# Second norm's sum of squares: the seventh tile's squares join the running sum

## The chip, the cores and the metric

The kernel runs on one core of one Trainium2 chip. The core has five engines that run side by side and meet through semaphores: TensorE (PE; its weight loads are shown apart, as PEld), VectorE (DVE), ScalarE (ACT), GpSimd (POOL) and SyncE (SP), which issues the DMAs here. The metric is the device time of one execution in microseconds; the time of a kernel is the median of its runs.

## The reference: what is computed

One decoder layer of depth 1 on 1024 tokens with 1024 features: an RMS norm, sliding-window attention with sinks, a residual add, a second RMS norm, a squared-ReLU MLP (hidden width 4096), another residual add and a final norm. What the change touches is the second norm, the one ahead of the MLP:

```python
def rms_norm(x, g):
    xf = x.astype(jnp.float32)
    y = xf * lax.rsqrt(jnp.mean(xf * xf, axis=-1, keepdims=True) + RMS_EPS)
    return (y * g.astype(jnp.float32)).astype(x.dtype)
...
        h = h + mix
        h = h + squared_relu_mlp(rms_norm(h, mlp_norm[i]), mlp_w_up[i], mlp_w_down[i])
```

For each token the mean of its 1024 squared features is wanted.

## The kernel before, in words

Features lie on the 128 partitions, tokens along the free axis. The residual `h` is eight tiles of 128 features by 1024 tokens, `h[0]` to `h[7]`, and is worked on in two halves of 512 tokens: half 0 and half 1. Big matrix products are made with operands split into a high and a low part, so one 128x512 block of a product is a run of matmuls in groups of three.

Around the change the program goes like this. The second part of the attention's output projection is made block by block (`oblock(m, hf)`, 12 matmuls each): first m = 0 to 7 for half 0, then m = 0 to 7 for half 1. After each block `oadd` (VectorE) adds it to `h[m]`, and `square` (ScalarE) writes the squares of that 128x512 piece into a tile `sq2_m_hf` (`sq` in the profile). The squares have to be summed over 1024 features, that is over the eight tiles and over the 128 partitions of each. Over tiles they are partly summed by adds into the first tile's squares: on VectorE for half 0, on GpSimd for half 1. Before the change the tiles 1 to 5 are added in this way, and the tiles 6 and 7 stand by themselves, so that `stat["sq", hf]` has three entries: the sum of tiles 0 to 5, tile 6, tile 7. The rest of the sum is made on TensorE: for each entry and each of the half's four token blocks, a matmul of 128 squares columns against one column of ones adds into the PSUM tile `n2s`. These small matmuls are not issued in a row. `stat_part` appends them to the list `tiny`, and the helper `mm` pops one of them after each big matmul that it issues. `stat_sum` empties the list, then `rstd` makes the reciprocal root from `n2s` (ScalarE's square root, five small VectorE operations, all on `n_st`), and `diag` makes the tile `dg` (VectorE). `stat_bcast` is a matmul of `dg` with ones that spreads the reciprocal root over all partitions (`n2b`).

For half 0 the small matmuls run inside block `oblock(0, 1)`, the first one of half 1, and `n2b` stands after `oblock(1, 1)`. With it VectorE scales half 0 (`x`, `xb`). For half 1 they run inside the MLP's first products: `up_mms(1, 0, ...)` appends them after its first three matmuls, `up_mms(2, 0, ...)` holds `stat_sum(1)`, and `up_mms(1, 1, ...)` holds `stat_bcast(1)`, each after its first group of three. With this `n2b` VectorE scales half 1 in place (`second_half`) and makes the sums `ta`, `xt` and so on of the MLP's fast product scheme. Between the product (1, 0) and the statistics ScalarE has `snapshot(1, 0)`, the copy `oa<-uX`.

GpSimd's work right behind its adds for half 1 is `up_sums_inplace(2, ...)`, four adds and subtractions of weights (`wu2c`, `s`, `wu2b`, `wu2c`).

The order on TensorE is the order of the program everywhere; on VectorE, ScalarE and GpSimd it is the order of the program from the start of half 1's loop on (`ordered = True`), and a scheduler's for the loop of half 0. Every engine instruction is recorded under line 41, the helper that wraps the engines, so groups are told by their tiles.

Of the kernel before, what the change touches and what calls it, by code (L numbers as in the profile page):

```python
# [62 lines left out]
def trunk(tc, xT, gains, wqkv, wo, wup, wdn, bias_d, sinks_d, ident_d, mask_d, outT):  # L63
# [29 lines left out]
    def rtile(name):  # L93
        return big.tile([P, 1024], F32, tag="R", name=name, bufs=3)
# [510 lines left out]
    def bank(tag, name):  # L605
        if tag == "mm":
            return mmtile(name)
        return pml.tile([P, 512], F32, tag=tag, name=name, bufs=BANKS[tag])
# [4 lines left out]
    def two(tile_):  # L613
        return tile_.rearrange("p (a c) -> p a c", a=2)
# [4 lines left out]
    def sqtile(name):  # L619
        return mlp.tile([P, 512], F32, tag="sq", name=name, bufs=4)  # L620
# [15 lines left out]
    def mm3b(ps, w, x, c, first, last):  # L636

        (wh, wl), (xh, xl) = w, x
        c = slice(c * P, c * P + P)
        mm(ps, wh[:, c], xh, first, False, skip_group_check=True)  # L640
        mm(ps, wh[:, c], xl, False, False, skip_group_check=True)
        mm(ps, wl[:, c], xh, False, last, skip_group_check=True)
# [5 lines left out]

    def stat_part(hf, i):

        first, last = (i == 1, i == 0) if hf == 0 else (i == 0, i == 2)
        if first:
            stat["ps", hf] = bank("Y", f"n2s{hf}")
        ps, sq = stat["ps", hf], stat["sq", hf][i]
        for b in range(4):
            tiny.append(lambda b=b: pe.matmul(
                ps[:, b:b + 1], lhsT=sq[:, b * P:(b + 1) * P], rhs=ones[:, 0:1], start=first and b == 0,
                stop=last and b == 3, skip_group_check=True))

    def stat_sum(hf):  # L660
        while tiny:
            tiny.pop(0)()
        rn2 = rstd(stat["ps", hf], 4, f"n2_{hf}")
        dg = sqtile(f"dg2_{hf}")
        diag(rn2, 0, 4, dg)
        stat["dg", hf] = dg

    def stat_bcast(hf):
        ps = bank("Y", f"n2b{hf}")
        bcast(4, ps, stat.pop(("dg", hf)))  # L670
        return ps

    def square(m, hf):
        sl = HALVES[hf]
        sq = sqtile(f"sq2_{m}_{hf}")
        s.activation(sq, h[m][:, sl], AF.Square)
        parts = stat.setdefault(("sq", hf), [])
        if m in (0, 6, 7):
            parts.append(sq)
        else:  # L680
            (v if hf == 0 else g).tensor_tensor(parts[0], parts[0], sq, op=ALU.add)
# [9 lines left out]
    def his(src, alloc, name):  # L691

        hi, lo = two(alloc(F32R, f"{name}_h")), two(alloc(F32R, f"{name}_l"))
        s.copy(hi, src)

        def los():
            v.tensor_tensor(lo, src, hi.bitcast(F32), op=ALU.subtract)
            return [(hi[:, i], lo[:, i]) for i in range(2)]

        return los  # L700

    def his1(src, alloc, name):
        x = two(alloc(F32R, name))
        s.copy(x[:, 0], src)

        def los():
            v.tensor_tensor(x[:, 1], src, x[:, 0].bitcast(F32), op=ALU.subtract)
            return x[:, 0], x[:, 1]

        return los  # L710

    def first_half(i, rb):
        xt = temp(f"x1_{i}")
        scaled(xt, i, 0, rb)
        x1.append(xt)
        return his(xt, qtile, f"xb{i}")

    def stored(i, hf):
        for m in (2 * i, 2 * i + 1):
            nc.sync.dma_start(hd[m][:, HALVES[hf]], h[m][:, HALVES[hf]])  # L720
# [67 lines left out]
    def up_load(p):  # L788
        raw, rw = two(rtile(f"wu{p}c")), two(rtile(f"wu{p}b"))
        nc.sync.dma_start(raw, wup[p, 0])  # L790
        nc.sync.dma_start(rw, wup[p, 1])
        return raw, rw
# [18 lines left out]
    def up_mms(n, p, hooks={}):  # L811
        wn, xn = TERM[n]
        key = {1: "X", 6: "X", 7: "X", 4: "X", 2: "Z", 5: "Y", 3: "Y"}[n]
        first, last = n in (1, 2, 5), n in (4, 2, 3)
        if first:
            tag = {(1, 3): "mm", (2, 1): "mm", (2, 2): "Y"}.get((n, p), key)
            PS[key, p] = bank(tag, f"u{key}{p}")
        for i in range(4):
            mm3b(PS[key, p], WU[wn, p], XP[xn, i], i, first and i == 0, last and i == 3)
            if i in hooks:  # L820
                hooks[i]()
# [8 lines left out]
    def snapshot(n, p):  # L830
        if n == 1:
            OUT["a", p] = two(pptile(F32, f"oa{p}"))
        else:
            OUT["b", p] = temp(f"ob{p}")
        s.copy(OUT["a" if n == 1 else "b", p][:, 0], PS["X", p])
# [68 lines left out]
    def oblock(m, hf):  # L904
        ps = bank(obanks[(hf * KT + m) % 5], f"o1_{m}_{hf}")
        for kk in range(4):
            mm3(ps, wsl(ws[m // 2], (m % 2) * 4 + kk), o_t[4 + kk], HALVES[hf], kk == 0, kk == 3)
        return ps

    def oadd(m, hf, ps):  # L910
        v.tensor_tensor(h[m][:, HALVES[hf]], ps, h[m][:, HALVES[hf]], op=ALU.add)
        square(m, hf)
# [5 lines left out]
    rb = None  # L918
    for m in range(KT):
        if m == 0:  # L920
            for i in (1, 2, 0):
                stat_part(0, i)
        ps = oblock(m, 1)
        if m == 0:
            stat_sum(0)
        if m == 1:
            rb = stat_bcast(0)
        if 2 <= m < 5:
            LO[m - 1] = first_half(m - 1, rb)
        if 2 <= m < 6:  # L930
            XP["b11", m - 2], XP["b21", m - 2] = LO[m - 2]()
        if m in (3, 4):
            WU["a22", m - 3] = LO["wb", m - 3]()
        oadd(m, 1, ps)
        if m == 0:
            for i in range(4):
                stored(i, 0)
            wu3 = two(rtile("wu3a"))
            nc.sync.dma_start(wu3, wup[3, 0])
        if m == 1:  # L940
            LO[0] = first_half(0, rb)
        if m in (1, 2):
            LO["wb", m - 1] = his1(SUM[m - 1][0][:, 1], wtile, f"wb{m - 1}")
        if m == 4:
            u2 = up_load(2)
        if m == 5:
            LO["ws0"] = his(SUM[0][1], wtile, "ws0")
        if m % 2 == 1:
            stored(m // 2, 1)
    s2_2 = up_sums_inplace(2, *u2)  # L950
    LO["wa3"] = his(wu3, wtile, "wa3")
    WU["s2", 0], WU["s1", 0] = LO["ws0"]()
    up_mms(1, 0, {0: lambda: [stat_part(1, i) for i in range(3)]})
    snapshot(1, 0)
    WU["a11", 3], WU["a12", 3] = LO["wa3"]()
    bc = []
# [339 lines left out]
```

## Time and profile before

| | us |
|---|---|
| median of three runs | 928.64 (928.47 to 928.67) |
| profiled execution, its own time | 926.65 |
| span of the profiled execution | 924.9 |
| TensorE busy in the span | 907.9 (98%) |
| VectorE busy | 692.6 (75%) |
| ScalarE busy | 447.2 (48%) |
| GpSimd busy | 280.3 (30%) |
| chain that ended last, TensorE's share | 89% |
| chain that ended last, VectorE's share | 7% |

A row of the timeline gives the start in us from the span's beginning, the duration, the engine, the line, the operation, what it writes and reads, its shape and a count (several alike in a row are merged); in brackets stand the idle time of the engine before it and what ended that. A row of the chain of waits gives the start, the duration, the engine and the tile. A row by windows gives, after the window and its length, the busy time and count of PE, PEld, DVE, ACT and POOL, and then TensorE's granted clock, the DMA share and GB/s. Matmuls are pipelined and overlap in the rows, so TensorE's pace is read from the starts of its weight loads.

### The profile page before, as it was taken

The page shows a single profiled execution, that of the slowest core. Times are in us where ns is not written, and L with a number is a line of the kernel's source. Part 1 is how long each engine was busy: PE and PEld are TensorE (multiplying, and loading weights), DVE is VectorE, ACT ScalarE, POOL GpSimd, SP SyncE. Part 2 cuts the span into 40 slices and gives each one's busy share as a digit, 9 for nine tenths or more (in the row PEclk, how much of TensorE's full clock was granted, in tenths as well). Part 3 has the DMA queues.
Part 4 walks back from the last instruction along what each step waited for, and adds up shares of the span by engine and source line. Part 5 has one row for each costly group of instructions (what it writes and reads, how often), then busy time and mean ns, then how long its engine had stood idle before and what let it go on. Part 6 is the DMA issues. An engine that isn't in the chain of part 4 may idle for free.

```text
span 924.9 us, 12585 instructions
## 1 busy us (share of the span) xinstructions
PE 907.9 (98%) x4504; PEld 764.8 (83%) x4504; DVE 692.6 (75%) x963; ACT 447.2 (48%) x857; POOL 280.3 (30%) x247
## 2 busy tenths in 40 slices
PE   8899999999999999999999999999999999999996
PEld 7788888888888778888888888788888888888995
DVE  7789988999858998877565665566877886568953
ACT  8588878777534474343333333343342434345511
POOL 1026656566255006653554434110000000040200
PEclk9999999999999999999999999999999999999997
DMA  8200100501454035645434454889888998448522
GB/s 314 69 29 29 53 29 8 210 25 45 124 188 145 1 119 192 220 141 171 170 125 148 150 177 151 299 314 409 293 332 292 341 327 324 151 160 285 189 92 91
DMA packets 57438, 160.36 MB, mean 173 GB/s; under 512 B 6432, under 2 KB 10272, under 8 KB 57376
## 3 DMA queue, kind: packets, MB, share of 16 engines
q1 hardware_dynamic: 57088, 159.42, 48.4%
q8 instruction: 35, 0.57, 0.3%
q14 instruction: 27, 0.22, 0.1%
q10 hardware_dynamic: 288, 0.14, 0.1%
HBM read 121.79 MB, written 37.75 MB: 172 GB/s over the span
## 4 chain that ended last, share of the span: by engine, by line
PE 89%; DVE 7%; ACT 2%; issue 1%; DMA 0%; DVEq 0%; ACTq 0%
PE d L41 33%; PE uX L41 16%; PE f L41 12%; PE uY L41 9%; PE o L41 5%; PE uZ L41 4%; PE pv L41 3%; PE S L41 3%; PE pt L41 1%; PE psv L41 1%; PE psk L41 1%; DVE h L41 1%; DVE ta L41 1%; DVE xt_l L41 1%; DVE oa L41 0%
## 5 line engine op out<-in xcount | busy, mean ns | idle before, releaser
L41 PE MATMUL d<-dx_h,dw_h 128*128 128x512 f32 (+1 forms) x512 | 186.4, 364 | 0.0
L41 PE MATMUL d<-dx_l,dw_h 128*128 128x512 f32 (+1 forms) x512 | 185.6, 363 | 0.0
L41 PE MATMUL d<-dx_h,dw_l 128*128 128x512 f32 (+1 forms) x512 | 185.6, 363 | 0.0
L41 PEld LDWEIGHTS d<-dx_h,dw_h 128*128 128x128 f32 x512 | 96.6, 189 | 15.4 <-issue 0.2
L41 PEld LDWEIGHTS d<-dx_l,dw_h 128*128 128x128 f32 x512 | 96.6, 189 | 15.2 <-issue 0.2
L41 PEld LDWEIGHTS d<-dx_h,dw_l 128*128 128x128 f32 x512 | 96.6, 189 | 14.9
L41 ACT CAST dw_h<-wf 128x1024 fp32r<-128x1024 f32 x40 | 41.9, 1051 | 95.7 <-PE d L41 80.1
L41 DVE TENSOR_TENSOR dx_l<-hr,dx_h 128x1024 fp32r<-128x1024 f32 x56 | 72.1, 1292 | 16.6 <-ACT dx_h L41 16.6
L41 ACT CAST dx_h<-hr 128x1024 fp32r<-128x1024 f32 x56 | 58.4, 1049 | 44.8 <-DMA hr<-hid 43.4
L41 POOL TENSOR_TENSOR ssq3a<-ssq3a,sq_a 128x512 f32<-128x512 f32 x7 | 11.7, 1665 | 209.5 <-ACT sq_a L41 209.1
L41 DVE TENSOR_TENSOR dw_l<-wf,dw_h 128x1024 fp32r<-128x1024 f32 x40 | 49.6, 1242 | 23.7 <-ACT dw_h L41 23.6
L41 POOL TENSOR_TENSOR t<-t,sm 128x512 f32<-128x512 f32 x32 | 33.3, 1040 | 108.5 <-DVE sm L41 108.5
L41 DVE TENSOR_TENSOR wf<-wd,we 128x1024 f32<-128x1024 f32 x40 | 49.3, 1248 | 20.1 <-DMA we<-wdn 10.9
L41 ACT ACTIVATE t<-t,sm 128x129 f32<-128x129 f32 x128 | 50.5, 397 | 11.1 <-DVE sm L41 10.6
L41 POOL TENSOR_TENSOR oc<-oc,oa 128x512 f32<-128x512 f32 x16 | 21.7, 1355 | 106.7 <-DVE oc L41 106.7
L41 PE MATMUL f<-xh,w_h 128*128 128x512 f32 x128 | 52.9, 413 | 0.0
L41 PE MATMUL f<-xl,w_h 128*128 128x512 f32 x128 | 50.2, 393 | 0.0
L41 PE MATMUL f<-xh,w_l 128*128 128x512 f32 x128 | 50.2, 392 | 0.0
L41 ACT COPY oa<-uX 128x512 f32<-128x512 f32 x32 | 18.8, 586 | 60.8 <-PE uX L41 60.8
L41 POOL TENSOR_TENSOR ob<-ob,oa 128x512 f32<-128x512 f32 x16 | 24.2, 1512 | 78.8 <-DVE ob L41 72.8
L41 PE MATMUL uX<-xu_h,wb 128*128 128x512 f32 x128 | 42.2, 391 | 0.7 <-ACT oa L41 0.7
L41 POOL TENSOR_SCALAR_AFFINE_SELECT cur<-hl 128x1024 fp32r<-128x1024 f32 x32 | 39.5, 1233 | 2.0 <-DVE hl L41 2.0
(372 smaller groups left out, 2388.9 us busy)
## 6 DMA issues: line engine op xcount, KB each, us to landing
wd<-wdn SPq DMA_DIRECT2D x56, 512.0 KB, 5.9
hr<-hid SPq DMA_DIRECT2D x56, 512.0 KB, 5.1
we<-wdn SPq DMA_DIRECT2D x40, 512.0 KB, 7.3
hid<-oa SPq DMA_DIRECT2D x32, 256.0 KB, 2.4
hid<-oc SPq DMA_DIRECT2D x32, 256.0 KB, 2.4
hid<-ob SPq DMA_DIRECT2D x32, 256.0 KB, 2.2
w_r<-wqkv SPq DMA_DIRECT2D x8, 512.0 KB, 3.9
h<-xT SPq DMA_DIRECT2D x8, 512.0 KB, 6.6
```

Of the source, the lines that this page charges most:

```text
L41: ins = method(*args, **kw)
```

## The change

The seventh tile (m = 6) is added to the running sum like the tiles 1 to 5, on VectorE for half 0 and on GpSimd for half 1. Two entries are left, the sum of tiles 0 to 6 and tile 7, so `stat_part` is called twice for each half and not three times. Half 0 takes them in the order (1, 0), tile 7 first; half 1 in the order 0, 1, the sum first.

```diff
     def stat_part(hf, i):
 
-        first, last = (i == 1, i == 0) if hf == 0 else (i == 0, i == 2)
+        first, last = (i == 1, i == 0) if hf == 0 else (i == 0, i == 1)
         if first:
             stat["ps", hf] = bank("Y", f"n2s{hf}")
         ps, sq = stat["ps", hf], stat["sq", hf][i]
...
         parts = stat.setdefault(("sq", hf), [])
-        if m in (0, 6, 7):
+        if m in (0, 7):
             parts.append(sq)
         else:
             (v if hf == 0 else g).tensor_tensor(parts[0], parts[0], sq, op=ALU.add)
...
         if m == 0:
-            for i in (1, 2, 0):
+            for i in (1, 0):
                 stat_part(0, i)
...
-    up_mms(1, 0, {0: lambda: [stat_part(1, i) for i in range(3)]})
+    up_mms(1, 0, {0: lambda: [stat_part(1, i) for i in range(2)]})
```

TensorE at the start of `oblock(0, 1)`, where half 0's small matmuls stand between the big ones. In the names, `sq_6_0` are the squares of tile 6 in half 0, `sq_0_0` the running sum; the number behind is a buffer's. Before:

```order
L41 MATMUL o_0_1_3148<-oh_1887,wo_0_h 128x512
L41 MATMUL n2s_3147<-ones,sq_6_0_3129 128x1
L41 MATMUL o_0_1_3148<-ol_1888,wo_0_h 128x512
...
L41 MATMUL o_0_1_3148<-ol_2196,wo_0_h 128x512
L41 MATMUL n2s_3147<-ones,sq_7_0_3145 128x1
L41 MATMUL o_0_1_3148<-oh_2195,wo_0_l 128x512
...
L41 MATMUL o_0_1_3148<-oh_2484,wo_0_l 128x512
L41 MATMUL n2s_3147<-ones,sq_0_0_3028 128x1
L41 MATMUL o_0_1_3148<-oh_2752,wo_0_h 128x512
```

and with the change:

```order
L41 MATMUL o_0_1_3149<-oh_1887,wo_0_h 128x512
L41 MATMUL n2s_3148<-ones,sq_7_0_3146 128x1
L41 MATMUL o_0_1_3149<-ol_1888,wo_0_h 128x512
...
L41 MATMUL o_0_1_3149<-ol_2196,wo_0_h 128x512
L41 MATMUL n2s_3148<-ones,sq_0_0_3028 128x1
L41 MATMUL o_0_1_3149<-oh_2195,wo_0_l 128x512
...
L41 MATMUL o_0_1_3149<-oh_2484,wo_0_l 128x512
L41 MATMUL o_0_1_3149<-oh_2752,wo_0_h 128x512
```

The small matmuls on tile 7 have moved from the fifth place to the first, right behind the first big matmul of the block; the last four big matmuls have none between them any more.

GpSimd behind half 1's adds, before and with the change:

```order
L41 TENSOR_TENSOR sq_0_1_3183<-sq_0_1_3183,sq_4_1_3299 128x512
L41 TENSOR_TENSOR sq_0_1_3183<-sq_0_1_3183,sq_5_1_3321 128x512
L41 TENSOR_TENSOR wu2c<-wu2c,wu2b 128x512
L41 TENSOR_TENSOR s_2_3363<-wu2b,wu2c 128x512
L41 TENSOR_TENSOR wu2b<-wu2b 128x512
```

```order
L41 TENSOR_TENSOR sq_0_1_3180<-sq_0_1_3180,sq_4_1_3296 128x512
L41 TENSOR_TENSOR sq_0_1_3180<-sq_0_1_3180,sq_5_1_3318 128x512
L41 TENSOR_TENSOR sq_0_1_3180<-sq_0_1_3180,sq_6_1_3340 128x512
L41 TENSOR_TENSOR wu2c<-wu2c,wu2b 128x512
L41 TENSOR_TENSOR s_2_3361<-wu2b,wu2c 128x512
L41 TENSOR_TENSOR wu2b<-wu2b 128x512
```

One add stands between the old last one and the weights' sums, which have moved one place back. On VectorE one add, of tile 6's squares in half 0, stands in the same way between the residual adds of tiles 6 and 7.

TensorE in the product (1, 0) (`uX`), at the end of half 1's small matmuls, before and with the change:

```order
L41 MATMUL n2s_3376<-ones,sq_6_1_3343 128x1
L41 MATMUL uX_3372<-xb_h,wa_l 128x512
L41 MATMUL n2s_3376<-ones,sq_7_1_3359 128x1
L41 MATMUL uZ_3398<-xb_h,wa_h 128x512
L41 MATMUL n2s_3376<-ones,sq_7_1_3359 128x1
L41 MATMUL uZ_3398<-xb_l,wa_h 128x512
```

```order
L41 MATMUL n2s_3374<-ones,sq_7_1_3357 128x1
L41 MATMUL uX_3370<-xb_l,wa_h 128x512
L41 MATMUL n2s_3374<-ones,sq_7_1_3357 128x1
L41 MATMUL uX_3370<-xb_h,wa_l 128x512
L41 MATMUL uZ_3395<-xb_h,wa_h 128x512
L41 MATMUL uZ_3395<-xb_l,wa_h 128x512
```

The last small matmul stood among the `uZ` matmuls of the next product; it now stands ahead of the last `uX` matmul.

## The prediction

> **What bounds the kernel now.** I read the chain of waits first, then TensorE's weight loads with their waits, then the rows around the two sums. The chain's rows are start, duration, engine and tile.
>
> ```profile
> 300.63 1.04 PE n2b L41 x2
> 301.69 1.41 DVE h L41 x2
> ...
> 346.32 5.76 PE uY L41 x24
> ...
> 603.35 275.51 PE d L41 x1272
> ```
>
> Up to the broadcast `n2b` of the second half, TensorE's own stream sets the end. Then the chain runs on VectorE from 301.69 to 346.32: VectorE starts when `n2b` lands and is the late engine for 45 us. From 346.32 to the end it is TensorE again. So one instant counts: when the second `n2b` lands. Whatever moves 301.69 moves the end alike. TensorE, where it waits in between, waits for VectorE, last and longest at 346.32:
>
> ```profile
> 346.32 0.19 PEld L41 LDWEIGHTS uY<-xt_h,ws_l 128*128 128x128 f32 x1 [1.42 <-DVE ob L41]
> ```
>
> **What the change removes.** Four one-column matmuls per half, each in the row of weight loads as two passes (x2) between big matmuls:
>
> ```profile
> 261.84 0.19 PEld L41 LDWEIGHTS o<-ol,wo_h 128*128 128x128 f32 x1
> ...
> 265.69 0.19 PEld L41 LDWEIGHTS o<-oh,wo_h 128*128 128x128 f32 x1
> 265.92 0.41 PEld L41 LDWEIGHTS n2s<-ones,sq 128*128 128x128 f32 x2
> 266.25 0.19 PEld L41 LDWEIGHTS o<-ol,wo_h 128*128 128x128 f32 x1
> 266.37 0.42 PEld L41 LDWEIGHTS n2s<-ones,sq 128*128 128x128 f32 x2
> ...
> 270.90 0.42 PEld L41 LDWEIGHTS n2s<-ones,sq 128*128 128x128 f32 x2
> ```
>
> 17 big loads take 265.69 - 261.84 = 3.85 us, 0.227 each. Ten steps of big plus small take 270.90 - 266.37 = 4.53, 0.453 each. A small one therefore costs 0.227; four save 0.91 us in each half, 1.81 in all. TensorE sets the time at both places, so this is real. It is also the most the change can gain.
>
> **What it adds in the first half.** One VectorE add, and a new head of the line: the first small matmul now reads tile 7's squares, not tile 6's.
>
> ```profile
> 264.18 0.63 ACT L41 ACTIVATE sq<-h 128x512 f32<-128x512 f32 x1 [2.09 <-DVE h L41]
> 266.90 0.63 ACT L41 ACTIVATE sq<-h 128x512 f32<-128x512 f32 x1 [2.09 <-DVE h L41]
> ...
> 253.72 0.68 DVE L41 TENSOR_TENSOR sq<-sq,sq 128x512 f32<-128x512 f32 x1
> ...
> 266.12 0.69 DVE L41 TENSOR_TENSOR h<-o,h 128x512 f32<-128x512 f32 x1 [2.03 <-PE o L41]
> ```
>
> The add is free: tile 6's squares end at 264.18 + 0.63 = 264.81, an add takes 0.68, so it ends near 265.5 inside VectorE's 2.03 us of idleness before 266.12; without that cover it would delay tile 7 by its 0.68. Not free is the wait. Tile 7's squares end at 266.90 + 0.63 = 267.53. Before, the four loads on tile 6 covered that (the fifth came at 267.72). Now the first load, due at 265.92, waits until about 267.58 (0.05 for the signal, as from 292.33 to 292.38 below): 1.66 us, with the other eleven big matmuls of the block queued behind it, and VectorE's next residual add waiting for those. A stalled TensorE restarts tighter; the second half shows it, since it has such a wait already:
>
> ```profile
> 292.38 0.30 PEld L41 LDWEIGHTS n2s<-ones,sq 128*128 128x128 f32 x2 [0.42 <-POOL sq L41]
> 292.60 0.19 PEld L41 LDWEIGHTS uX<-xb_l,wa_h 128*128 128x128 f32 x1
> 292.71 0.43 PEld L41 LDWEIGHTS n2s<-ones,sq 128*128 128x128 f32 x2
> ...
> 297.25 0.42 PEld L41 LDWEIGHTS n2s<-ones,sq 128*128 128x128 f32 x2
> ```
>
> From 292.38 to the next small load is 0.33, not 0.45, so 0.12 comes back: 1.66 - 0.12 = 1.54. First half: +1.54 - 0.91 = **+0.63 us**. The sums themselves end a little earlier than before (eight steps from 267.58 instead of twelve from 265.92), so the first `n2b` does not wait. It only stands 0.63 later in TensorE's order, and VectorE, which starts its scaling on it, shifts with it, and so does GpSimd behind it. Below I keep the old times and add 0.63 at the end.
>
> **What it adds in the second half.** One GpSimd add on the path: the first small load needs the finished sum, which now includes tile 6.
>
> ```profile
> 291.74 1.20 ACT L41 ACTIVATE sq<-h 128x512 f32<-128x512 f32 x2
> ...
> 291.03 1.30 POOL L41 TENSOR_TENSOR sq<-sq,sq 128x512 f32<-128x512 f32 x1 [0.31 <-ACT sq L41]
> 292.30 2.26 POOL L41 TENSOR_TENSOR wu2c<-wu2c,wu2b 128x512 f32<-128x512 f32 x1
> 294.63 2.14 POOL L41 TENSOR_TENSOR s<-wu2b,wu2c 128x512 f32<-128x512 f32 x1
> 296.74 1.27 POOL L41 TENSOR_TENSOR wu2b<-wu2b 128x512 f32<-128x512 f32 x1
> 297.98 1.28 POOL L41 TENSOR_TENSOR wu2c<-wu2c,s 128x512 f32<-128x512 f32 x1
> ...
> 292.13 1.28 DVE L41 TENSOR_TENSOR ws_l<-sa,ws_h 128x1024 fp32r<-128x1024 f32 x1
> 293.90 1.74 DVE L41 TENSOR_TENSOR wa_l<-wu3a,wa_h 128x1024 fp32r<-128x1024 f32 x1 [0.49 <-ACT wa_h L41]
> 298.37 0.91 DVE L41 TENSOR_TENSOR n_st<-n_st 128x4 f32<-128x4 f32 x1
> ```
>
> Tile 6's squares end at about 292.36, half of the 1.20; GpSimd is free at 292.33. The new add starts near 292.4 to 292.5, exactly where `wu2c` stood. How long it takes is the main unknown. Alone, such a GpSimd operation takes 1.27 to 1.30. In this slot it took 2.26, ending 294.56: about one operation's length after VectorE's `ws_l` (two operands in SBUF) ended at 293.41. Then `wa_l` on VectorE stretched until it outlasted `wu2c`, and `s` stretched behind `wa_l`: they take turns, whole instructions at a time. The add of 291.03, beside a VectorE add from PSUM, was not stretched. I take 2.26's end, since place, shape and neighbour are the same: the sum is ready at 294.56, the first load at 294.60 instead of 292.38, **+2.22**. The lower bound is 1.30: end 293.8, +1.47. Less than 1.27 is nowhere in these rows, so no gain is possible here.
>
> TensorE's own place at the second `n2b` moves by 2.22 - 0.91 = +1.31. The statistics must also arrive by then.
>
> ```profile
> 296.32 0.59 ACT L41 COPY oa<-uX 128x512 f32<-128x512 f32 x1 [2.45 <-PE uX L41]
> 297.80 0.26 ACT L41 ACTIVATE n_st<-n2s,eps 128x4 f32<-128x4 f32 x1 [0.89 <-PE n2s L41]
> ...
> 299.78 0.69 DVE L41 TENSOR_TENSOR dg<-ident,n_st 128x512 f32<-128x512 f32 x1
> 301.69 1.41 DVE L41 SCALAR_TENSOR_TENSOR h<-h,gn,n2b 128x512 f32<-128x512 f32 x2 [1.22 <-PE n2b L41]
> ...
> 273.89 0.42 PEld L41 LDWEIGHTS n2b<-dg,ones 128*128 128x128 f32 x2
> ...
> 275.19 2.73 DVE L41 SCALAR_TENSOR_TENSOR x<-h,gn,n2b 128x512 f32<-128x512 f32 x4 [0.17 <-PE n2b L41]
> ...
> 300.02 0.19 PEld L41 LDWEIGHTS uX<-xb_h,wa_l 128*128 128x128 f32 x1
> 300.53 0.30 PEld L41 LDWEIGHTS n2b<-dg,ones 128*128 128x128 f32 x2 [0.32 <-DVE dg L41]
> ```
>
> Before, `n2b` was due at 300.02 + 0.23 = 300.25 and waited for `dg` until 300.53. Now it is due at 300.25 + 1.31 = 301.56. ScalarE's square root stands behind the copy `oa`. Eight small matmuls end before the last `uX` matmul, so the copy, at 296.32 + 2.22 = 298.54, comes first, and the root starts near 299.1 rather than 297.80. The `n_st` product on VectorE is then issued at about 299.65 (298.37 - 297.80 later) and meets GpSimd's last operation, one slot later than before (one more operation of about 1.28, so until 300.57), as it met one before (0.91 for four columns, ending at 299.28 just as `wu2c` ended). From its end to `n2b` was 300.53 - 299.28 = 1.25, so `n2b` comes at about 301.83: **+1.30**. If it meets nothing, `n2b` goes when due, at 301.56. VectorE started 1.30 after an unstalled load (273.89 to 275.19) and 1.16 after a stalled one (300.53 to 301.69), so it starts at 302.86: +1.17.
>
> **Sum.** 0.63 + 1.30 = +1.93 us (1.80 with the free `n_st`). The stretch after 301.69 repeats itself, later by that much. The four GpSimd sums, 0.63 + 1.3 later, are first read by ScalarE's cast of `s`,
>
> ```profile
> 324.37 0.62 ACT L41 CAST ws_h<-s 128x512 fp32r<-128x512 f32 x1
> ```
>
> 25 us after the last of them ends (299.26), so their delay costs nothing; without that cover it would cost those 1.9. No DMA is added, and none stands in another place of SyncE's queue. The profiled execution took 926.65 (span 924.9), which becomes 928.6. The median of the runs is 1.99 above it, so 928.64 becomes **930.6**.
>
> **The Trainium skill on the pair.** "SBUF — State Buffer", section "Who interferes with whom", says that a VectorE instruction with two SBUF inputs and a GpSimd one that reads SBUF exclude each other, and that issue order decides who waits. The rows above agree (2.26 behind `ws_l`). By it, an add issued ahead of `ws_l` would cost its 1.30 alone, which is the first rival's price.
>
> **Rivals.** *Not blocked, hence not measurably slower*: the GpSimd add gets in ahead of `ws_l` or runs beside it. For it: of the five adds of this kind in the half, whose row (least, median and most in ns) is
>
> ```profile
> L41 POOL TENSOR_TENSOR sq<-sq,sq x5: 1292/1297/1421, 275.8 to 291.0; 128x512 f32<-128x512 f32 x5
> ```
>
> none was blocked for long. Against: `ws_l` starts at 292.13, before tile 6's squares exist. Then the load comes at 293.85, +1.47 - 0.91 = +0.56, `n2b` is due at 300.81, VectorE starts at 302.11, +0.42; with 0.63 it is +1.05: 929.7. It decides if the add starts before `ws_l`.
>
> *Slower still*: GpSimd loses its turn twice, behind `wa_l` too (1.1 more), or the lag in VectorE's chain grows by such an operation: 0.63 + 1.30 + 1.1 = +3.0, 931.7. Against: `wa_l` waits for its cast until 293.90, and the add is then in its turn.
>
> *The clock*: TensorE idles 1.7 and 2.2 us and restarts slow. One block of 12 big matmuls (2.7 us) at half rate at each place would add 5.4: about 936. Against it is this window, which holds the longest wait, 2.14:
>
> ```profile
> 43.95 0.14 PEld L41 LDWEIGHTS vt<-ident,vT 128*128 128x128 f32 x1 [2.14 <-DVE vv L41]
> ...
> 42.00:45.00 3.00, 1.30 (x8) 0.87 (x7) 2.34 (x6) 1.21 (x3) 0.00 (x0) 1.00 0.00 0
> ```
>
> The granted clock (third from the right) stayed 1.00. The Trainium skill, "TensorE: Matmul & The Clock Gate", section "What's actually happening", puts the fall to half rate at an idle window of about 3.4 us; by it two stalls of 1.7 and 2.2 would cost nothing more, as the row has it.
>
> *Faster*: the waits vanish and only the savings stay, 1.81 us: 926.8. For it: nothing but other timing; tile 7's squares would have to end 1.6 us sooner.
>
> **How the numbers follow.** 0.2%, about what a measurement of this kernel can tell from no change, is 1.86 us, 930.50. Main case 0.71, its own range 930.1 to 931.0, just over half of it above 930.50; not blocked 0.15; slower still 0.08; clock 0.02; faster 0.04, hardly beyond 0.2% even in full. Slower: 0.40 + 0.08 + 0.02 = 0.50; faster 0.03; the rest, 0.47, within. The range, 929.5 to 931.4, takes in the unblocked add and reaches towards the slower case.
>
> **What would show it.** A wait of about 1.66 us ahead of the first `n2s` load, for ScalarE's `sq`; the second-half wait grown from 0.42 to about 2.6 for GpSimd's `sq`, whose last add takes over 2 us; 32 `n2s` loads instead of 48; the square root behind the copy; VectorE's chain begun 1.9 us later, and ended so. The forecast is wrong if the sixth add takes 1.3, if the first wait is not there, or if TensorE's wait at 346.32 shrinks instead of moving.

## The result and the profile after

| | before | after |
|---|---|---|
| median of 16 runs each, one chip | 928.35 us | 933.34 us |
| lowest and highest | 926.61, 929.20 | 928.29, 935.18 |
| ratio, 95% interval | | 1.0052 [1.0040, 1.0064] |
| profiled execution, its span | 926.65, 924.9 | 935.15, 933.4 |

The change makes the kernel slower, by 0.5%. That is 5.0 us where 2.0 were forecast, and the median lies outside the range of 929.5 to 931.4. The runs of the changed kernel also spread more, in four groups: two at 928.3 to 928.4, four at 929.7 to 930.5, six at 932.7 to 933.6, four at 934.7 to 935.2. Before, there were two: six runs at 926.6 to 927.0 and ten at 928.1 to 929.2. Two executions among the experiments below, near 1300 us at a mean clock of 0.65 (one of half 1 alone, one with the wait filled), stand apart from all others and are left out.

Where the time stands in the profiled execution is told by its chain of waits (start, duration, engine, tile):

```profile
310.18 1.41 DVE h L41 x2
...
354.80 5.74 PE uY L41 x24
...
611.82 275.51 PE d L41 x1272
```

Against 301.69, 346.32 and 603.35 before, each is 8.5 us later, as is the end of the span. So all of it was lost ahead of the second `n2b`, and nothing was lost or regained behind it. The timeline of TensorE's weight loads in the changed kernel shows the two forecast waits, and then something else:

```profile
269.52 0.30 PEld L41 LDWEIGHTS n2s<-ones,sq 128*128 128x128 f32 x2 [1.70 <-ACT sq L41]
...
269.85 0.42 PEld L41 LDWEIGHTS n2s<-ones,sq 128*128 128x128 f32 x2
...
297.17 0.44 PEld L41 LDWEIGHTS n2s<-ones,sq 128*128 128x128 f32 x2 [2.62 <-POOL sq L41]
...
297.70 0.76 PEld L41 LDWEIGHTS n2s<-ones,sq 128*128 128x128 f32 x2
...
298.56 0.76 PEld L41 LDWEIGHTS n2s<-ones,sq 128*128 128x128 f32 x2
...
303.68 0.33 PEld L41 LDWEIGHTS uZ<-xb_h,wa_h 128*128 128x128 f32 x1
304.11 0.33 PEld L41 LDWEIGHTS uZ<-xb_l,wa_h 128*128 128x128 f32 x1
...
307.52 0.19 PEld L41 LDWEIGHTS uZ<-xb_h,wa_h 128*128 128x128 f32 x1
307.75 0.19 PEld L41 LDWEIGHTS uZ<-xb_l,wa_h 128*128 128x128 f32 x1
...
308.88 0.42 PEld L41 LDWEIGHTS n2b<-dg,ones 128*128 128x128 f32 x2
```

Behind the second wait a step of one big and one small matmul takes 298.56 - 297.70 = 0.86 us, where it took 0.45 in half 0 and before. Two big loads stand 0.43 apart until 307.5 and 0.23 from then on. The view by windows of the same kernel shows what goes with it; the third number from the right is the granted clock:

```profile
294.00:297.00 3.00, 0.97 (x5) 0.47 (x3) 2.41 (x3) 2.45 (x4) 2.83 (x2) 1.00 0.77 295
297.00:300.00 3.00, 2.83 (x11) 2.54 (x11) 1.20 (x1) 0.00 (x0) 2.92 (x3) 0.54 0.24 81
300.00:303.00 3.00, 3.00 (x13) 2.71 (x12) 0.00 (x0) 0.00 (x0) 3.00 (x3) 0.50 0.27 100
303.00:306.00 3.00, 3.00 (x9) 2.42 (x9) 0.73 (x5) 0.75 (x2) 0.13 (x1) 0.50 0.00 0
306.00:308.00 2.00, 2.00 (x8) 1.53 (x7) 0.69 (x1) 0.00 (x0) 0.00 (x0) 0.62 0.00 0
```

In the trace's record of the clock it falls to 0.50 at 297.26 and returns at 307.50. Those 10.24 us at half speed do the work of some 5.12, an estimate from the clock alone. In the page's slices of 23 us this shows only as one 8 in the middle of a row of nines.

The 8.49 us in parts, by weight loads: the first `n2s` load of half 0 is 3.60 later (269.52 against 265.92), which is the wait forecast at 1.66, and most of the rest is 1.7 from a shorter fall of the clock, at 44.68 for 3.41 us, ahead of which nothing was changed (more on it below):

```profile
42.00:45.00 3.00, 1.30 (x6) 0.82 (x5) 2.40 (x5) 1.49 (x4) 0.00 (x0) 0.95 0.00 0
45.00:48.00 3.00, 3.00 (x9) 2.22 (x9) 0.81 (x3) 0.77 (x3) 0.00 (x0) 0.50 0.00 0
```

From half 0's first `n2s` load to half 1's it is 1.19 more (27.65 against 26.46), the forecast 2.22 - 0.91 - 0.12. From half 1's first `n2s` load to the `n2b` load it takes 308.88 - 297.17 = 11.71 instead of 8.15. The prediction had that stretch shrink by the 0.91 of four small matmuls; it grew by 3.56. The remaining 0.14 is the longer way from an unstalled `n2b` load to VectorE.

### The profile page after: what moved, and what is told of

Read it like the earlier page. It is cut to its first block, busy times and chain, and to the rows that moved or that the text cites. A ratio compares the mean times of both kernels' runs of the same rounds, so it can differ in the third digit from the quotient of the medians.

```text
span 933.4 us, 12556 instructions
## 1 busy us (share of the span) xinstructions
PE 913.7 (98%) x4488; PEld 769.0 (82%) x4488; DVE 693.0 (74%) x964; ACT 447.3 (48%) x857; POOL 279.3 (30%) x248
## 4 chain that ended last, share of the span: by engine, by line
PE 88%; DVE 8%; ACT 2%; issue 1%; DMA 0%; POOL 0%; DVEq 0%; SPq 0%; POOLq 0%; ACTq 0%
PE d L41 33%; PE uX L41 16%; PE f L41 13%; PE uY L41 8%; PE uZ L41 4%; PE pv L41 3%; PE o L41 3%; PE S L41 3%; PE pt L41 1%; DVE x L41 1%; DVE h L41 1%; PE psv L41 1%; PE psk L41 1%; DVE xb_l L41 1%; DVE ta L41 1%
```

## The experiments

The theory from these rows: the waits cost what was forecast, and beyond that the 2.6 us wait lets the granted clock fall. The rival: something else in the change costs 5 us, and the clock follows from it. Each kernel below has its own runs of the kernel before beside it, on its chip.

### One half at a time

The change in half 0 alone (the first and second edits below), and in half 1 alone (the third to fifth):

```diff
-        if m in (0, 6, 7):
+        if m in (0, 7) or (m == 6 and hf == 1):
...
-            for i in (1, 2, 0):
+            for i in (1, 0):
```

```diff
-        first, last = (i == 1, i == 0) if hf == 0 else (i == 0, i == 2)
+        first, last = (i == 1, i == 0) if hf == 0 else (i == 0, i == 1)
...
-        if m in (0, 6, 7):
+        if m in (0, 7) or (m == 6 and hf == 0):
...
-    up_mms(1, 0, {0: lambda: [stat_part(1, i) for i in range(3)]})
+    up_mms(1, 0, {0: lambda: [stat_part(1, i) for i in range(2)]})
```

> The change in half 0 alone; half 1 keeps its three parts. Theory A (the wait in half 1, 2.6 us long, is what lets the granted clock fall; the wait in half 0, 1.7 us, does not): +0.6 us over the kernel before in nearly all executions, no stretch at clock 0.50 between 260 and 350 us, n2s waits of 1.7 (for ScalarE) and 0.4 (for GpSimd). Theory B (any added wait, or the thinner row of small matmuls, lowers the clock): some executions 3 to 5 us longer than the others, and a stretch at 0.50 behind 270 us.

> The change in half 1 alone; half 0 keeps its three parts. Theory A: +1.3 us in the executions whose clock stays at 1.00 and about 5 more in more than half of them, so a median of +4 to +6 and a spread of 5 to 7 us. Theory B: half of the whole change's cost, +2 to +3.

Half 0 alone: 927.66 (927.12 to 930.22), ratio 1.0006 [0.9998, 1.0015]. The kernel before has two groups in this job too, 926.2 to 927.4 and 928.0 to 929.0; seven of the eleven runs lie 0.8 above the lower one's middle. Half 1 alone: 932.90, ratio 1.0047 [1.0032, 1.0062]; of nine runs seven lie at 932.2 to 934.7, one at 927.69 and one at 929.42. So nearly all of the 5 us are half 1's. The timelines, of half 0 alone

```profile
270.02 0.30 PEld L41 LDWEIGHTS n2s<-ones,sq 128*128 128x128 f32 x2 [1.70 <-ACT sq L41]
...
270.35 0.42 PEld L41 LDWEIGHTS n2s<-ones,sq 128*128 128x128 f32 x2
```

and of half 1 alone:

```profile
296.90 0.30 PEld L41 LDWEIGHTS n2s<-ones,sq 128*128 128x128 f32 x2 [2.62 <-POOL sq L41]
...
297.23 0.68 PEld L41 LDWEIGHTS n2s<-ones,sq 128*128 128x128 f32 x2
...
298.00 0.76 PEld L41 LDWEIGHTS n2s<-ones,sq 128*128 128x128 f32 x2
```

In these profiles the 1.70 wait is followed by full speed, the 2.62 wait by half speed.

### The wait filled

The whole change, with ten throwaway 128x512 matmuls into `n2s`'s bank ahead of half 1's first small one (which clears what they wrote), so that TensorE does not idle while GpSimd adds:

```diff
-        if first:
+        if first and hf == 0:
...
-    up_mms(1, 0, {0: lambda: [stat_part(1, i) for i in range(2)]})
+    def keep_busy(n):
+        stat["ps", 1] = bank("Y", "n2s1")
+        for _ in range(n):
+            pe.matmul(stat["ps", 1], lhsT=WU["a11", 0][0][:, 0:P], rhs=XP["b11", 0][0], start=True, stop=True,
+                      skip_group_check=True)
+
+    up_mms(1, 0, {0: lambda: [keep_busy(10)] + [stat_part(1, i) for i in range(2)]})
```

> The whole change, and ten extra 128x512 matmuls (operands of the product running there, result thrown away) ahead of half 1's first small matmul: they fill 2.27 of the 2.6 us for which TensorE idles, and delay nothing by more than 0.1. Theory A: no fall of the clock behind 297 us, +1.9 us over the kernel before, executions no further apart than those of the kernel before. Theory B: as slow as the whole change, about +5.

It took 929.86 (928.56 to 932.40), ratio 1.0026 [1.0017, 1.0035]. From the timeline of this kernel:

```profile
292.56 2.23 PEld L41 LDWEIGHTS n2s<-xb_h,wa_h 128*128 128x128 f32 x10
...
295.38 0.30 PEld L41 LDWEIGHTS n2s<-ones,sq 128*128 128x128 f32 x2 [0.36 <-POOL sq L41]
...
295.71 0.42 PEld L41 LDWEIGHTS n2s<-ones,sq 128*128 128x128 f32 x2
...
300.38 1.04 DVE L41 TENSOR_TENSOR n_st<-n_st 128x4 f32<-128x4 f32 x1
...
302.66 0.30 PEld L41 LDWEIGHTS n2b<-dg,ones 128*128 128x128 f32 x2 [0.36 <-DVE dg L41]
...
303.82 1.41 DVE L41 SCALAR_TENSOR_TENSOR h<-h,gn,n2b 128x512 f32<-128x512 f32 x2 [1.22 <-PE n2b L41]
```

GpSimd's sum and the first small load come no earlier, once the 1.7 us that the changed kernel's profiled execution lost near 45 us are taken off its 297.17. But the clock stays at 1.00 until the last 8 us of the span, and the stretch from that load to `n2b`'s takes 7.28 us instead of 11.71. TensorE does more work here than in the changed kernel, and yet on the same chip the kernel is 3.0 us faster than half 1's part alone (929.86 against 932.90), though half 0's part is in it too. That decides against the rival: with the idle time filled, the fall of the clock behind it is gone from the profile, and its price with it.

This execution, the shortest of its ten, also comes close to the main case of the forecast, free of that fall: VectorE's chain begins 2.13 us later than before (303.82 against 301.69), for a forecast sum of 1.93. That the span is longer by just 1.9 (926.8 against 924.9) is luck, since the end of the program gave 0.2 back (below). Seven of the other nine runs lie 1.1 to 2.0 us above this one and one 3.8, more than the 2.8 over which the kernel before spreads here. That part of the expectation failed, and no profile shows where those runs lost their time.

### A shorter wait in half 1

Half 1 alone, with the small matmuls one or two groups of three big ones later:

```diff
-    up_mms(1, 0, {0: lambda: [stat_part(1, i) for i in range(2)]})
+    up_mms(1, 0, {1: lambda: [stat_part(1, i) for i in range(2)]})
```

(`{2: ...}` in the second.)

> The change in half 1 alone, with the small matmuls put in one group of three big matmuls later: the same GpSimd add is waited for, but TensorE has 0.68 us more to do ahead of it, so it idles about 1.9 us and not 2.6. Theory A (the clock falls when enough of one fixed period of 3.4 us is idle): still some slow executions, fewer than with 2.6 (where 17 of 25 were slow): 20 to 45 in 100. In the others +0.4 us over the kernel before, since the second n2b is due at 300.9 and its statistics come at 300.5 as before. Theory C (any idle longer than some fixed bound, whatever the period): all or none.

> As before it, two groups later: TensorE idles about 1.3 us. Theory A: no execution with a fall behind 290 us, and no cost left, 0.0 to +0.2 us over the kernel before: the second n2b is due at 300.2 and waits for its statistics until 300.5 as it does in the kernel before. If the blocked GpSimd add itself costs (not only TensorE's wait): +1 or more.

One group later: 928.73 (927.32 to 933.25), ratio 1.0019 [1.0006, 1.0032], with two of twelve runs at 933 and two at 930.3 to 930.9. Two groups later: 928.88 (927.71 to 929.77), ratio 1.0012 [1.0003, 1.0020], none above 930. Long falls become rarer with the wait, as expected (two of twelve for a forecast of 20 to 45 in a hundred), but both kernels are slower than expected. The timeline of the first:

```profile
294.91 0.30 PEld L41 LDWEIGHTS n2s<-ones,sq 128*128 128x128 f32 x2 [1.94 <-POOL sq L41]
...
299.08 0.62 DVE L41 TENSOR_TENSOR n_st<-n_st 128x4 f32<-128x4 f32 x1
299.74 1.42 DVE L41 SCALAR_TENSOR_TENSOR n_st<-n_st 128x4 f32<-128x4 f32 x2
...
302.00 0.30 PEld L41 LDWEIGHTS n2b<-dg,ones 128*128 128x128 f32 x2 [0.87 <-DVE dg L41]
```

The small operations on `n_st`, 0.16 and 0.36 where nothing is in their way, now take 0.62 and 1.42 beside GpSimd's four sums, which stand one place later behind the added sum. In the second kernel they take 1.06 and 1.39, and its profile, against the expectation, has a fall of the clock of one period. Its view by windows:

```profile
294.00:297.00 3.00, 2.19 (x15) 2.03 (x16) 1.71 (x1) 0.68 (x2) 2.97 (x2) 1.00 0.15 29
297.00:300.00 3.00, 3.00 (x14) 2.50 (x14) 1.70 (x4) 0.26 (x1) 2.95 (x3) 0.67 0.43 160
300.00:303.00 3.00, 3.00 (x11) 2.08 (x9) 1.66 (x3) 0.00 (x0) 0.79 (x1) 0.76 0.00 0
```

Its wait is only 1.27. I had taken that as too short; that step of the theory fell.

### Other orders of the two parts

In half 0 the sum could go first and tile 7 last, since the sum of seven tiles is ready when the block begins. First alone, half 1 staying at three parts; then with the whole change, and in half 1 tile 7 first and the sum last:

```diff
-        first, last = (i == 1, i == 0) if hf == 0 else (i == 0, i == 2)
+        first, last = (i == 0, i == 1) if hf == 0 else (i == 0, i == 2)
...
-        if m in (0, 6, 7):
+        if m in (0, 7) or (m == 6 and hf == 1):
...
-            for i in (1, 2, 0):
+            for i in (0, 1):
```

```diff
-        first, last = (i == 1, i == 0) if hf == 0 else (i == 0, i == 1)
+        first, last = (i == 0, i == 1) if hf == 0 else (i == 1, i == 0)
...
-            for i in (1, 0):
+            for i in (0, 1):
...
-    up_mms(1, 0, {0: lambda: [stat_part(1, i) for i in range(2)]})
+    up_mms(1, 0, {0: lambda: [stat_part(1, i) for i in (1, 0)]})
```

> Half 0 in two parts with the sum of tiles 0 to 6 first and tile 7 second; half 1 keeps three parts. The sum is ready near 265.5, before the first small matmul is due, and four small matmuls cover tile 7's squares. Both theories: no wait for ScalarE there, -0.9 us. If the step on the order of the operands is wrong (the cost lies in the added VectorE add): +0.3 or more.

> The whole change with the entries taken in the other order: half 0 the sum first and tile 7 second, half 1 tile 7 first and the sum second. Theory A: no wait above 1.1 us at either place, no fall of the clock there; half 0 gives 0.9 us, half 1 between 0 (if the n_st product meets a GpSimd operation as before) and 1.2: -0.9 to -2.1 us over the kernel before. Theory B (two parts as such slow the clock): slower than the kernel before.

The first took 926.05 (925.31 to 928.06), ratio 0.9988 [0.9979, 0.9996]: the saving of four small matmuls without the wait. The second took 927.09, ratio 0.9997 [0.9988, 1.0005]: no wait for GpSimd, no fall in the profile but the one at the very end, eight small matmuls fewer, and no measurable gain, a miss. Its timeline, of three engines, shows who took it:

```profile
292.53 0.30 PEld L41 LDWEIGHTS n2s<-ones,sq 128*128 128x128 f32 x2 [1.02 <-ACT sq L41]
...
296.44 1.29 POOL L41 TENSOR_TENSOR s<-wu2b,wu2c 128x512 f32<-128x512 f32 x1
297.69 1.29 POOL L41 TENSOR_TENSOR wu2b<-wu2b 128x512 f32<-128x512 f32 x1
298.94 1.28 POOL L41 TENSOR_TENSOR wu2c<-wu2c,s 128x512 f32<-128x512 f32 x1
...
297.79 2.45 DVE L41 SCALAR_TENSOR_TENSOR n_st<-n_st 128x4 f32<-128x4 f32 x2
...
301.09 0.30 PEld L41 LDWEIGHTS n2b<-dg,ones 128*128 128x128 f32 x2 [1.67 <-DVE dg L41]
```

Two four-column operations take 2.45 us instead of 0.36, one GpSimd operation each, and `n2b` waits 1.67.

### Why the kernel before has two groups of times

TensorE waits 2.14 us ahead of a transposition of v near 44 us. In the profile of half 0 alone the clock falls right there, for one period (third number from the right):

```profile
42.00:45.00 3.00, 1.17 (x6) 0.70 (x6) 2.84 (x7) 1.73 (x4) 0.00 (x0) 0.98 0.00 0
45.00:48.00 3.00, 3.00 (x10) 2.21 (x10) 0.77 (x3) 0.74 (x2) 0.00 (x0) 0.50 0.00 0
```

The kernel before, with four and eight throwaway matmuls ahead of the third and fourth transposition:

```diff
+        if n in (2, 3):
+            idle = patt.tile([P, 4, 256], F32, tag="S", name=f"idle{n}", bufs=2)
+            for _ in range({2: 4, 3: 8}[n]):
+                pe.matmul(idle[:, 0:2].rearrange("p a b -> p (a b)"), lhsT=ones_r, rhs=dg1[0][:, 0:512],
+                          start=True, stop=True)
         ps = small(("pt", "pv")[n % 2], f"vt{n}")
```

> The kernel before, with twelve extra 128x512 matmuls (result thrown away) in the two waits of the attention's start, ahead of the third and fourth transposition of v (1.1 and 2.1 us idle at 41.2 and 44.0 us). Theory A: the executions of the kernel before fall into two groups, 926.7 and 928.3, because this 2.1 us wait lets the clock fall for one period in half of them; filled, all fall into the lower group or up to 0.4 above it, 926.6 to 927.2. If the two groups have another cause (the start, the end): both groups stay.

It took 926.37, with eleven runs between 926.21 and 927.34: the upper group is gone, as the theory has it, though no execution of that group was profiled. Ratio 0.9990 [0.9981, 0.9999]. The four groups of the changed kernel then read as no fall (928.3), the short one (1.7 more), the long one (5.1 more) and both (6.8 more); its profiled execution, of the highest group, has both. The same edit on the changed kernel, and together with half 0's better order:

> The whole change, with the throwaway matmuls ahead of the third and fourth transposition of v, so that only the wait of 2.6 us in half 1 is left as a place for the clock to fall. Theory (two independent places, one of them now gone): two groups in place of four, near 926.4 + 1.6 = 928.0 without the fall and 933 with three periods at half clock; at the 17 of 25 seen so far the median is near 933. Rival (the fall in half 1 is tied to what happened at the v transposition): always or never, one group.

> The kernel before with two edits that each helped alone: half 0 in two parts with the sum first and tile 7 behind it (half 1 stays at three parts), and throwaway matmuls on TensorE ahead of the third and fourth transposition of v, where it otherwise waits. Alone they gave 926.05 and 926.37 against medians of 927.24 to 927.29. Theory (the first saves TensorE's work ahead of the second n2b, the second keeps the granted clock at 1.00; the two do not touch): 926.37 less what half 0 saved within each group of the kernel before (0.75 to 0.9) gives 925.5 to 925.6, in one group, with no fall of the clock in the profile. Rival (what half 0 gained was itself a rarer fall of the clock): no better than 926.1 to 926.4.

On the changed kernel: 935.06, all five runs at 933.5 to 935.35, ratio 1.0085 [1.0071, 1.0099]. The profiled run, 933.5, has the fall of 10.24 us and nothing near 45. No run at 928 appeared, which five runs do not rule out; so the rival, that the fall now comes always, stays open. The four runs at 934.65 and above are higher than that one fall explains; their mean clock is lower still (0.988 to 0.989 against 0.990), but none of them was profiled. Both gains on the kernel before: 926.06, ratio 0.9986 [0.9977, 0.9995], no better than half 0's order alone, a miss. From its timeline:

```profile
297.91 0.49 DVE L41 TENSOR_TENSOR n_st<-n_st 128x4 f32<-128x4 f32 x1
298.43 1.42 DVE L41 SCALAR_TENSOR_TENSOR n_st<-n_st 128x4 f32<-128x4 f32 x2
...
300.69 0.30 PEld L41 LDWEIGHTS n2b<-dg,ones 128*128 128x128 f32 x2 [0.95 <-DVE dg L41]
```

The clock holds, TensorE is early, and it waits 0.95 for statistics that took turns with GpSimd. Half 0's better order, with or without the filled transpositions, is the best version found: it beats the kernel before by 0.1% and so, by the two ratios (0.9988 and 1.0052), the changed one by some 0.6%.

### The same wait with dense work behind it

Half 1 alone, the first small matmul where it was, the other seven held back behind nine big ones; then the same with the throwaway matmuls at the transpositions:

```diff
-    up_mms(1, 0, {0: lambda: [stat_part(1, i) for i in range(2)]})
+    rest = []
+
+    def first_alone():
+        stat_part(1, 0)
+        rest.extend(tiny[1:])
+        del tiny[1:]
+
+    def others():
+        tiny.extend(rest)
+        stat_part(1, 1)
+
+    up_mms(1, 0, {0: first_alone, 3: others})
```

> The change in half 1 alone, with the first small matmul where it was, so that its wait stays at about 2.6 us, but the other seven held back: nine big matmuls run without any between them behind the wait, then three with small ones between, then the last four small ones in a row. Theory (the clock falls at the end of a period in which TensorE was mostly idle, and comes back after a period without gaps or small matmuls): a fall of one period of 3.41 us, worth 1.7 us, in place of three periods and 5.1 us; the executions lie at about 928 without it, and 929.5 to 931.3 with it, median near 930. Rival one (the wait alone sets the length of the fall): 10.24 us at half clock, a median near 932.9 as with the change in half 1 alone. Rival two (the small matmuls behind the wait are needed for the fall): no fall, a median of 928 to 928.5.

> The change in half 1 alone, with the wait of 2.62 us kept and dense big matmuls behind it, and with the throwaway matmuls ahead of the v transpositions, so that the wait in half 1 is the only place left for a fall of the clock. It asks what the spread of 928.5 to 930.9 without these throwaways was. Theory one (the wait alone never lets the clock fall; the thin row is needed): one group, near 928.2 (928.51, the run whose profile shows no fall anywhere, less the 0.3 that the throwaways gave the kernel before's lower group), mean clock 0.996 or more in every run. Theory two (the wait alone lets it fall for one period in some executions): a second group 1.7 us higher, near 929.9, with a mean clock near 0.994. Either way nothing at 932 or above.

The first: 929.72, seven runs at 928.51 to 930.92, ratio 1.0026 [1.0015, 1.0037]. The second: 929.39, ratio 1.0025 [1.0014, 1.0037], with two runs at 928.2 to 928.3, eight at 929.1 to 929.8, and two at 932.69 and 933.68, where neither theory had any. The profiled run of the first, by windows and by its wait:

```profile
294.00:297.00 3.00, 1.34 (x7) 1.17 (x8) 2.20 (x2) 0.94 (x2) 3.00 (x2) 1.00 0.29 107
297.00:300.00 3.00, 3.00 (x22) 2.70 (x21) 0.00 (x0) 0.59 (x1) 2.92 (x3) 1.00 0.55 169
```

```profile
295.66 0.30 PEld L41 LDWEIGHTS n2s<-ones,sq 128*128 128x128 f32 x2 [2.62 <-POOL sq L41]
```

So a wait of 2.62 does not always bring the clock down. With the thin row of small matmuls behind it, 22 of 30 runs lie 4 us or more above where their kernel lies without a fall (10 of 16, 7 of 9 and 5 of 5, the last against the 928 expected); with dense work behind it, 2 of 19 do. The eight runs in the middle have a mean clock of 0.994 to 0.995 against 0.995 to 0.996 of the two lowest, which fits a fall of one period (1.7 us, of which `n2b`'s wait of 0.37 hides some); no profile of one of them exists, so this is argued, not shown.

### What the profiles say together

Every complete stretch at half clock in these profiles is a multiple of 3.413 us long, and the first boundary, kept on in steps of 3.413 through the whole trace, hits the later ones. So each trace has its grid of periods, and one can count, in each, the weight loads of big matmuls that began (those of `n2s` on the squares and of `n2b` are left out, the ten throwaway ones count). Fifteen or sixteen is a dense row at full clock, eight a dense row at half clock. Around half 1's wait, worked out from the traces:

| kernel | wait | big loads by period, from the one that holds most of the wait | clock in the periods after |
|---|---|---|---|
| after | 2.62 | 3, 4, 5, 8, 12 | 0.5, 0.5, 0.5, 1.0 |
| half 1 alone | 2.62 | 2, 4, 6, 8, 11 | 0.5, 0.5, 0.5, 1.0 |
| after, transpositions filled | 2.63 | 2, 4, 6, 8, 11 | 0.5, 0.5, 0.5, 1.0 |
| dense work behind the wait | 2.62 | 6, 10, 11, 10 | 1.0 throughout |
| the same, transpositions filled | 2.63 | 8, 8, 11, 14 | 1.0 throughout |
| one group later | 1.94 | 8, 7, 13, 9 | 1.0 throughout |
| two groups later | 1.27 | 10, 7, 8, 11 | 1.0, 0.5, 1.0 |
| wait filled | 0.36 | 8, 13, 11, 15 | 1.0 throughout |

The first five rows tell one story: a period that began 2 or 3 of 15 big matmuls is followed by half clock, one with 6 or 8 is not, and half clock lasts until a period is full. With small matmuls between them a half-clock period only fits 4 to 6 big ones, and in these traces it goes on; the one-period falls began 8 to 11 in theirs. That is how the thin row makes the fall three periods long. Half 0's wait of 1.70 left 6 or more in every period of the four profiles that have it, and none fell. In the fourth and fifth rows the wait lies across a boundary of the grid (295.12 and 293.36), in the first three within one period; these profiles alone do not tell whether that or the dense work kept the clock. The seventh row breaks the rule: it fell after 7 big and 16 small loads, where the row above, with 7 big and 14 small, did not. What the chip counts is therefore not quite the big loads, and where its threshold lies stays open.

TensorE's busy time in such a period, from windows laid on the grid, parts the cases at the transposition and in half 1 better than the loads do. The six periods at these two places that a fall followed, the seventh row's aside, hold 1.0 to 1.4 us of it. Those that kept the clock hold 1.7 or more. The seventh row is the exception here too: its period was busy for 3.2 us, about half of it with small matmuls (eight at 0.227 us).

Every profile has one more fall, which no experiment touched: as TensorE runs out of work, the clock goes to 0.50 for the last 6 to 9 us of the span. Some of these falls came after periods that were busy for 2 to 2.8 us, ending in small matmuls, so the line at 1.4 to 1.7 does not hold there. Where the fall comes ahead of the program's last two matmuls, `n3b`, these take longer. The kernel before (fall at 915.57), and the same with the transpositions filled (fall at 918.01):

```profile
916.88 1.22 PE L41 MATMUL n3b<-dg,ones 128*128 128x256 f32 x2 [1.66 <-DVE dg L41]
```

```profile
916.97 0.70 PE L41 MATMUL n3b<-dg,ones 128*128 128x256 f32 x2 [1.66 <-DVE dg L41]
```

So two executions can differ by half a microsecond at the end alone. It is all of the 0.4 by which the second of these is the shorter (span 924.5 against 924.9).

## Why the prediction was wrong, point by point

**What bounds the kernel, and the instant that counts**: right. 301.69, 346.32 and the end moved alike.

**What is removed, 0.91 for each half**: right where the clock held. Half 0's better order alone gained 0.8 in the lower group of runs and some 1.0 in the upper.

**Half 0, +0.63**: right. The wait was 1.70 for a forecast 1.66, the 0.12 came back (269.52 to 269.85 is 0.33), and the part alone cost 0.8.

**Half 1, the blocked add, +2.22, and the second `n2b`, +1.30**: right. The profile after, of GpSimd and ScalarE:

```profile
295.08 2.04 POOL L41 TENSOR_TENSOR sq<-sq,sq 128x512 f32<-128x512 f32 x1 [0.17 <-ACT sq L41]
297.07 2.26 POOL L41 TENSOR_TENSOR wu2c<-wu2c,wu2b 128x512 f32<-128x512 f32 x1
...
304.34 0.59 ACT L41 COPY oa<-uX 128x512 f32<-128x512 f32 x1 [7.89 <-PE uX L41]
304.82 0.27 ACT L41 ACTIVATE n_st<-n2s,eps 128x4 f32<-128x4 f32 x1
```

The add took over 2 us (the rule from the Trainium skill that the prediction weighed, "SBUF — State Buffer", "Who interferes with whom", holds here), the square root stands behind the copy, and with the wait filled the `n_st` product met GpSimd's last operation (1.04) and VectorE's chain began 2.13 later, for a sum of 1.93. The "not blocked" rival and "slower still" are out: one turn was lost, not none and not two.

**The clock, chance 0.02**: this is the step that failed. The sum put the clock at nothing, and it cost about 5 us behind half 1's wait in 10 of 16 runs, counted by their groups of times. Three things in it were wrong.

The argument against it was one window of one execution: a wait of 2.14 at a clock of 1.00. The same wait does drop the clock in the profiles of the changed kernel and of each half alone, which are alike at this place, and, by its two groups of times, in other executions of the kernel before. The numbers to suspect it stood in the prediction itself: "The median of the runs is 1.99 above it". I carried that gap along as a constant. It is mostly the 1.7 us of a period at half clock: the profiled execution was one of the lower group. In it the period around the transposition's wait began 8 loads and kept its clock; in the profile of half 0 alone it began 5 and lost it. (In between the loads are not sharp: 7 lost it in the changed kernel, 7 kept it in others; their busy times were 1.4 and 1.7 us.)

The wait that was weighed was also too short. The step speaks of stalls of 1.7 and 2.2 us, and 2.2 is only what the change adds to the second one. Its whole length, "about 2.6" by the prediction's own last paragraph, is beyond the 2.14 that was to cover it.

And the rule I leaned on did not carry that far. The Trainium skill, "TensorE: Matmul & The Clock Gate", section "What's actually happening", speaks of a window of 3413 ns that is free-running. The traces agree, to the 3.413 us of each fall. But I took its "idle window" for an idle gap of that length, so that 2.2 us seemed safe. What the traces show is a decision on a fixed period in which TensorE need only be mostly idle: 2.62 us without work and three big matmuls were enough. The page does not say how busy is busy enough, and no sum could be made from it; the price of a period at half clock could: 1.7 us, and here there were three, 5.1 us. The rival's price, one block at half rate at each of two places, 5.4, was near the truth for the wrong reason: one place, and almost four times as long as a block, because, as the periods above read, the small matmuls kept the clock from returning.

**The chances**: with the clock at 0.02, "within" got 0.47. Fourteen of the sixteen runs of the changed kernel lie above 929.5 and ten of them above the range.

**What was to show it**: the two waits, the add over 2 us, 32 `n2s` loads and the root behind the copy all came; the chain of VectorE began and ended alike, but 8.5 us later in that execution and not 1.9. Signs that only confirm a mechanism do not show what else came with it.

## What to carry to other kernels

A stall on the engine that sets the time has two prices: its length, and the clock it may cost afterwards; judge the second by how much work a whole period of 3.4 us keeps, wherever the period happens to lie, and by whether dense work or thin work follows. A gap between the profiled execution and the median of the runs is a piece of evidence with a size; explain it before carrying it along. Work added on GpSimd is paid again by the short VectorE operations that it is pushed onto: look at who runs beside it after the shift.

## What was not expected of the hardware

- The clock came down after a wait of 2.62 us in a period of 3.413 us, and stayed down 10.24 us although TensorE had work in all of it; the profiled executions that had it lost some 5 us by it.
- Whether it falls depends, as the traces read, on where the grid of periods lies, and so differs between executions of one kernel. By the groups of times it fell in half 1 in ten of sixteen runs of the changed kernel, and at the transposition in ten of sixteen of the kernel before.
- Ten needless matmuls in the wait made the changed kernel faster: 1.0026 of the kernel before instead of 1.0052, some 2.4 us.
- Two four-column VectorE operations that otherwise take 0.36 us together took 1.39 to 2.45 beside GpSimd's 128x512 sums, and `n2b` waited 0.87 to 1.67 us for it in three kernels.
